# Later low parts, summed squares on TensorE, two scalings on ACT and pinned transposes in a two-layer trunk

## The chip, the cores and the metric

The kernel runs on one core of one Trainium2 chip. The metric is the device time of one execution in microseconds; of the kernel before, three runs were taken (2293.90, 2294.22 and 2296.38), and their median is 2294.22 us. A separate execution was profiled.

## The reference, cut to what matters

256 tokens of width 2048 go through two layers. Layer 0 mixes 8 heads of differential attention with 8 heads of a gated delta rule, layer 1 is a dilated attention with 16 heads; behind each stands an MLP of width 8192. All of it is float32.

```python
def l2_norm(x):                    # of q and k of the delta rule, per head of 128
    xf = x.astype(jnp.float32)
    return xf * lax.rsqrt(jnp.sum(xf * xf, axis=-1, keepdims=True) + NORM_EPS)

def squared_relu_mlp(h, w1, w2):
    return jnp.square(jax.nn.relu(h @ w1)) @ w2

for l in range(DEPTH):
    i = l // 2
    if l % 2 == 0:
        x = x + diff_delta_mixer(rms_norm(x, ab_norm[i]), l, ...)
    else:
        x = x + dilated_mixer(rms_norm(x, c_norm[i]), ...)
    x = x + squared_relu_mlp(rms_norm(x, mlp_norm[l]), mlp_w1[l], mlp_w2[l])
```

In the mixer of layer 0, `bq` and `bk` are normed by `l2_norm` before the delta rule, and the output of the attention is normed per head (`rms_norm(oa, a_sub_norm)`).

## The kernel before, in words

**The dense products.** `dense` (L191) computes one block of up to 512 output columns for both halves of the tokens (h = 0, 1; 128 tokens each) over 16 chunks of 128 input channels (8, 10 or 6 chunks in the output projections). Activations and weights are split into a high part, rounded to the format fp32r, and a low part, the rest; a product is high by high, high by low and low by high. So each chunk has six instructions on TensorE: for each h, L210 (`sh` by `wh`), L211 (`sh` by `wl`, the weights' low part) and L212 (`sl` by `wh`), all added up in one bank of PSUM per h. ACT makes `wh` by a copy (L204), DVE then makes `wl` by a subtraction (L107 through `tt`). With `unit=2`, in the MLPs, one cast and one subtraction serve two chunks; with `unit=1`, everywhere else, each chunk has its own. Six buffers of `wh` and `wl` exist at `unit=1`, three double ones at `unit=2`. Weights come by DMA on SP's queue, two chunks at a time (`wload`).

**The streams.** Everything that is not a dense product is written as generators in three streams ("g" for the delta rule, "s" for the rest, "o" for the outputs). After every chunk (or every second one), `drip` runs one step of one of them, g and s in turn, "o" after each fourth. `flush` runs the steps without dense products between them.

**The order on the engines.** A planner takes the instructions in program order as their priority (casts and subtractions of weights are moved forward by AHEAD = 60), estimates when operands and buffers are ready, and fixes the order of each engine's queue from that. An instruction on TensorE can so be placed before products that come earlier in the program, where the planner expects those to wait. `tc.issue_after(ins)` forbids that: each instruction written in its block, on the engine of `ins`, is placed behind `ins`. `behind` (L400) wraps each step of a generator so, behind the dense product written last (`last_mm`). Before the change it stands inside the first mixer and is used for the first transposes of x alone.

**The delta rule.** `gdn` (L617) runs four times (s = 0 to 3), each for two heads in two halves of the tokens, which makes four tiles of 128 x 128. It reads `qk`, with channels in the partitions. It transposes the four tiles of k and the four of q into two banks of PSUM (L631, recorded under L235); ACT squares each tile with a sum along the row (L634, recorded under L125) and copies k to `kh` (L636); DVE makes the reciprocal root (`rsqrt`), scales the four tiles of `kh` (L641, recorded under L117), and the decay matrix `dd` follows. Three yields later `kh` is transposed again (`kt`, L658).

**The attention's output.** `diff_out` (L838) norms a block of four tiles: squares and sums on ACT, `rsqrt` and four scalings on DVE (L842, under L117), then transposes (`out_T`).

**The transitions.** `next_norm` (L295) makes the sums of squares and the transposed, split blocks of x for the next stage, one call for each quarter n of the width. For n = 3 three yields lie between the sums and the transposes, so that they are written among the chunks of the next stage's first dense block. Three such transitions exist: into the first MLP (`xb`), into the mixer of layer 1 (`xc`) and into the second MLP (`xd`). At each, the pool with the weights' casts changes, and the first cast of the new stage waits for the last dense product of the old one.

Of the kernel before, what the change touches and what calls it, by code (L numbers as in the profile page):

```python
# [11 lines left out]
F32 = mybir.dt.float32  # L12
# [3 lines left out]
ALU = mybir.AluOpType  # L16
# [3 lines left out]
P = 128  # L20
# [67 lines left out]
def trunk(  # L88
# [32 lines left out]
    def act(o, a, f, scale=1.0, bias=0.0, accum=None):  # L121
        if accum is None:
            S.activation(out=o, in_=a, func=f, scale=scale, bias=bias)  # L123
        else:
            S.activation(out=o, in_=a, func=f, scale=scale, bias=bias, accum_out=accum)  # L125
# [4 lines left out]
    def ps_t(name):  # L130
        return pst.tile([P, 512], F32, tag="t", name=name)
# [4 lines left out]
    def quads(t, n=4):  # L136
        return t.rearrange("p (c d) -> p c d", c=n)
# [53 lines left out]
    def dense(wsrc, stat, kcs, nm, pre=(), every=1, unit=1):  # L191

        n = sum(s.shape[1] for s in wsrc)
        ps = [psd.tile([P, 512], F32, tag="d", name=f"{nm}p{h}") for h in range(NH)]
        first, last = kcs[0], kcs[-1]
        for j, kc in enumerate(kcs):
            if j % 2 == 0:
                raw = pre[j // 2] if j // 2 < len(pre) else wload(wsrc, kc, nm)
            if j % unit == 0:
                w = raw[:, j % 2:j % 2 + unit, :n]  # L200
                whs = wq[0].tile([P, unit, 512], F32R, tag="wh", name=f"{nm}h{kc}", bufs=6 // unit)[:, :, :n]
                wls = wq[0].tile([P, unit, 512], F32R, tag="wl", name=f"{nm}l{kc}", bufs=6 // unit)[:, :, :n]
                with tc.high_priority(offset=AHEAD):
                    cast[0] = S.copy(whs, w)  # L204
                    tt(wls, w, whs.bitcast(F32), ALU.subtract)
            wh, wl = whs[:, j % unit], wls[:, j % unit]
            for h in range(NH):
                sh, sl = stat(kc, h)
                o = ps[h][:, :n]
                E.matmul(o, lhsT=sh, rhs=wh, start=kc == first, stop=False)  # L210
                E.matmul(o, lhsT=sh, rhs=wl, start=False, stop=False)  # L211
                last_mm[0] = E.matmul(o, lhsT=sl, rhs=wh, start=False, stop=kc == last)  # L212
            if j % every == 0:
                drip()
        return ps
# [18 lines left out]
    def transpose(o, i, k=P):  # L234
        E.transpose(o, i, ident[:k, :k])  # L235
# [51 lines left out]
    def turn_quadrant(src, dst, i):  # L287
# [3 lines left out]
        for j in range(4):  # L291
            dv = dst[32 * j:32 * j + 32].rearrange("p c (h t) -> p h c t", h=NH)
            V.transpose(out=dv[:, :, :, q], in_=sv[:, :, :, j, :])  # L293

    def next_norm(n, norm, nm, dst, pool=None):  # L295

        stats_block(xs[n], n, nm + "s")
        if n == 3:
            for _ in range(3):
                yield  # L300
        yield from xt_block(xs[n], n, norm, nm, dst, pool if n < 3 else None)
        if n == 3:
            stats_end(nm + "e")
            yield
# [73 lines left out]
    with ExitStack() as mix:  # L378
# [16 lines left out]
        def xt_blocks():  # L395
            for n in range(4):
                for _ in xt_block(xq[n], n, 0, f"xa{n}", xb):
                    yield

        def behind(gen):  # L400

            while True:
                with tc.issue_after(last_mm[0].ins):
                    if next(gen, gen) is gen:
                        return
                yield

        blocks = xt_blocks()
        next(blocks)
# [207 lines left out]
        def gdn(qks, s, vb, nm):  # L617

            def mt(tag, n=4, share=None):
                return mp.tile([P, n, P], F32, tag="g_" + (share or tag), name=nm + tag)  # L620
# [2 lines left out]
                yield  # L623
            qk = qks[s]
            tiles = [(h, e) for h in range(NH) for e in range(2)]
            ssq = mp.tile([P, 8], F32, tag="g_ss", name=nm + "ss")
            kh = mt("kh")
            for w, o, c in (("k", 0, 2), ("q", 4, 0)):
                pt = ps_t(nm + w + "p")
                for i, (h, e) in enumerate(tiles):  # L630
                    transpose(pt[:, i * P:(i + 1) * P], qk[:, c + e, h * P:(h + 1) * P])  # L631
                j = sp.tile([P, 512], F32, tag="junk", name=f"{nm}j{o}")
                for i in range(4):
                    act(j[:, i * P:(i + 1) * P], pt[:, i * P:(i + 1) * P], AF.Square, accum=ssq[:, o + i:o + i + 1])  # L634
                if w == "k":
                    S.copy(kh, quads(pt))  # L636
            yield
            rs = mp.tile([P, 8], F32, tag="g_rs", name=nm + "rs")
            rsqrt(rs, ssq, 8, 1.0, nm)
            for i in range(4):  # L640
                ts(kh[:, i, :], kh[:, i, :], rs[:, i:i + 1], None, ALU.mult)  # L641
            sq = mp.tile([P, 4], F32, tag="g_sq", name=nm + "sq")
            ts(sq, rs[:, 4:8], 128.0 ** -0.5, None, ALU.mult)

# [5 lines left out]
                hd = 2 * s + e  # L650
                stt(dd[:, i, :], dd[:, i, :], gc[:, h, hd:hd + 1], cst("causal"), ALU.add, ALU.min)
            act(dd, dd, AF.Exp)
            for _ in range(3):
                yield
            khT, kd, kbg = mt("khT"), mt("kd", n=2), mt("kbg", n=2)
            t = ps_t(nm + "kt")
# [181 lines left out]
        def diff_out(o, s, nm):  # L838
            rs = mp.tile([P, 4], F32, tag="o_rs", name=nm + "ors")
            rsqrt(rs, out_ss(o, nm), 4, 1.0 / 128.0, nm + "o")  # L840
            for i in range(4):
                ts(o[:, i, :], o[:, i, :], rs[:, i:i + 1], None, ALU.mult)  # L842
            yield
            yield
            out_T(o, nm, oa, s, gsub)
            yield
# [355 lines left out]
```

## Time and profile before

| | before |
|---|---|
| median of three runs | 2294.22 us |
| the profiled execution's own time | 2293.58 us |
| its span, first to last instruction | 2291.8 us |
| TensorE (PE) busy, instructions | 2279.2 us, 10536 |
| weight loads (PEld) busy | 1887.6 us |
| VectorE (DVE) busy | 1670.6 us, 3027 |
| ScalarE (ACT) busy | 1195.0 us, 1865 |
| DMA, mean | 186 GB/s |

"Busy" is the share of the span in which an engine had an instruction in work. TensorE's instructions are pipelined: the record of a dense product is 0.39 us long, and the next one starts before it ends. What a product takes from the time is so read from the distance of two starts, in the timeline. A transpose is one record on TensorE; a product of float32 operands that are not rounded to fp32r is two records, each with a weight load of its own.

### The profile page before, as it was taken

The numbers are of one execution on the slowest core, as the hardware profiler recorded it, in microseconds if no ns is written. First come the engines' busy times: TensorE is split into PE (matmuls) and PEld (weight loads), VectorE is DVE, ScalarE is ACT, GpSimd is POOL, SyncE is SP. The second block draws the span as 40 slices with busy tenths as digits, with TensorE's granted clock in tenths as the row PEclk, the third lists the DMA queues.
The fourth block names the chain that finished last, engine by engine and source line by source line (L and its number), as shares of the span: only waits on it lengthen the run. The fifth ranks groups of instructions, "written<-read, shape, count | busy, mean of one in ns | idle before, by whom it ended". The sixth has DMA issues, their size and how long they took to land.

```text
span 2291.8 us, 29876 instructions
## 1 busy us (share of the span) xinstructions
PE 2279.2 (99%) x10536; PEld 1887.6 (82%) x10536; DVE 1670.6 (73%) x3027; ACT 1195.0 (52%) x1865; POOL 5.6 (0%) x15
## 2 busy tenths in 40 slices
PE   9999999999999999999999999999999999999999
PEld 8887888788888888888888888888888888888887
DVE  6868797867757746846888888986775775775774
ACT  6557666655534534534545565555543543543553
POOL 0000000000000000000000000000000000000000
PEclk9999999999999999999999999999999999999999
DMA  8655564456666666666656555555666666666665
GB/s 259 192 172 159 143 182 134 141 177 199 200 194 186 200 194 189 197 195 190 194 192 193 183 176 176 174 184 168 194 194 194 194 194 194 191 195 194 188 208 165
DMA packets 271546, 426.54 MB, mean 186 GB/s; under 512 B 22386, under 2 KB 102436, under 8 KB 271396
## 3 DMA queue, kind: packets, MB, share of 16 engines
q1 hardware_dynamic: 271220, 424.57, 61.3%
q8 instruction: 82, 1.34, 0.3%
q14 instruction: 68, 0.56, 0.1%
q10 hardware_dynamic: 176, 0.07, 0.0%
HBM read 420.11 MB, written 4.46 MB: 185 GB/s over the span
## 4 chain that ended last, share of the span: by engine, by line
PE 94%; DVE 3%; DMA 1%; ACT 1%; issue 1%; SPq 0%; ACTq 0%
PE m_0p L211 3%; PE n_2p L211 3%; PE n_1p L212 3%; PE n_0p L212 3%; PE m_3p L212 3%; PE m_3p L210 3%; PE m_2p L212 3%; PE m_2p L210 3%; PE m_1p L212 3%; PE m_1p L210 3%; PE n_0p L210 3%; PE n_1p L211 3%; PE n_2p L212 3%; PE m_0p L212 3%; PE n_2p L210 3%; PE n_1p L210 3%
## 5 line engine op out<-in xcount | busy, mean ns | idle before, releaser
L107 DVE TENSOR_TENSOR n_3l<-n_3r,n_3h 128x1024 fp32r<-128x1024 f32 x64 | 78.4, 1224 | 76.8 <-ACT n_3h L204 76.7
L107 DVE TENSOR_TENSOR n_2l<-n_2r,n_2h 128x1024 fp32r<-128x1024 f32 x64 | 78.4, 1224 | 76.8 <-ACT n_2h L204 76.7
L107 DVE TENSOR_TENSOR m_0l<-m_0r,m_0h 128x1024 fp32r<-128x1024 f32 x64 | 78.1, 1225 | 73.4 <-ACT m_0h L204 73.0
L107 DVE TENSOR_TENSOR n_1l<-n_1r,n_1h 128x1024 fp32r<-128x1024 f32 x64 | 78.4, 1224 | 67.7 <-ACT n_1h L204 66.9
L204 ACT CAST n_2h<-n_2r 128x1024 fp32r<-128x1024 f32 x64 | 67.5, 1054 | 100.2 <-PE n_2p L212 59.9
L204 ACT CAST n_3h<-n_3r 128x1024 fp32r<-128x1024 f32 x64 | 67.5, 1054 | 100.2 <-PE n_3p L212 59.9
L204 ACT CAST m_0h<-m_0r 128x1024 fp32r<-128x1024 f32 x64 | 67.1, 1054 | 97.2 <-PE m_0p L212 59.9
L204 ACT CAST n_1h<-n_1r 128x1024 fp32r<-128x1024 f32 x64 | 67.5, 1054 | 92.8 <-PE n_1p L212 59.9
L107 DVE TENSOR_TENSOR m_1l<-m_1r,m_1h 128x1024 fp32r<-128x1024 f32 x64 | 78.4, 1225 | 36.9 <-ACT m_1h L204 35.9
L204 ACT CAST m_1h<-m_1r 128x1024 fp32r<-128x1024 f32 x64 | 67.5, 1054 | 66.6 <-PE m_1p L212 38.3
L204 ACT CAST m_3h<-m_3r 128x1024 fp32r<-128x1024 f32 x64 | 67.5, 1054 | 57.3 <-PE m_3p L212 39.9
L204 ACT CAST n_0h<-n_0r 128x1024 fp32r<-128x1024 f32 x64 | 67.5, 1054 | 57.3 <-PE n_0p L212 39.9
L204 ACT CAST m_2h<-m_2r 128x1024 fp32r<-128x1024 f32 x64 | 67.5, 1054 | 57.3 <-PE m_2p L212 39.9
L107 DVE TENSOR_TENSOR n_0l<-n_0r,n_0h 128x1024 fp32r<-128x1024 f32 x64 | 78.4, 1225 | 25.8 <-ACT n_0h L204 24.0
L107 DVE TENSOR_TENSOR m_3l<-m_3r,m_3h 128x1024 fp32r<-128x1024 f32 x64 | 78.4, 1225 | 25.7 <-ACT m_3h L204 23.9
L107 DVE TENSOR_TENSOR m_2l<-m_2r,m_2h 128x1024 fp32r<-128x1024 f32 x64 | 78.4, 1225 | 25.7 <-ACT m_2h L204 23.7
L293 DVE STREAM_TRANSPOSE m_0hT<-m_0r 32x256 f32<-32x256 f32 x128 | 55.8, 436 | 5.8 <-ACT m_0r L123 3.7
L293 DVE STREAM_TRANSPOSE m_1hT<-m_1r 32x256 f32<-32x256 f32 x128 | 55.8, 436 | 5.7 <-ACT m_1r L123 3.6
L293 DVE STREAM_TRANSPOSE m_2hT<-m_2r 32x256 f32<-32x256 f32 x128 | 55.8, 436 | 5.7 <-ACT m_2r L123 3.6
L293 DVE STREAM_TRANSPOSE m_3hT<-m_3r 32x256 f32<-32x256 f32 x128 | 55.8, 436 | 5.7 <-ACT m_3r L123 3.6
L210 PE MATMUL n_0p<-n_0h,m_0hh 128*128 128x512 f32 x64 | 24.9, 389 | 0.0
L211 PE MATMUL n_0p<-n_0l,m_0hh 128*128 128x512 f32 x64 | 24.9, 389 | 0.0
(2553 smaller groups left out, 7388.3 us busy)
## 6 DMA issues: line engine op xcount, KB each, us to landing
m_0r<-in_mlp_w_dram SPq DMA_DIRECT2D x64, 512.0 KB, 4.2
m_1r<-in_mlp_w_dram SPq DMA_DIRECT2D x64, 512.0 KB, 3.8
m_2r<-in_mlp_w_dram SPq DMA_DIRECT2D x64, 512.0 KB, 4.2
m_3r<-in_mlp_w_dram SPq DMA_DIRECT2D x64, 512.0 KB, 3.8
n_0r<-in_mlp_w_dram SPq DMA_DIRECT2D x64, 512.0 KB, 4.2
n_1r<-in_mlp_w_dram SPq DMA_DIRECT2D x64, 512.0 KB, 4.2
n_2r<-in_mlp_w_dram SPq DMA_DIRECT2D x64, 512.0 KB, 4.3
n_3r<-in_mlp_w_dram SPq DMA_DIRECT2D x64, 512.0 KB, 4.3
```

The source lines that it names most:

```text
L107: V.tensor_tensor(out=o, in0=a, in1=b, op=op)
L204: cast[0] = S.copy(whs, w)
L210: E.matmul(o, lhsT=sh, rhs=wh, start=kc == first, stop=False)
L211: E.matmul(o, lhsT=sh, rhs=wl, start=False, stop=False)
L212: last_mm[0] = E.matmul(o, lhsT=sl, rhs=wh, start=False, stop=kc == last)
L293: V.transpose(out=dv[:, :, :, q], in_=sv[:, :, :, j, :])
```

## The change

Four things are changed. In `dense`, L211 leaves its place: for each chunk, both halves' L210 and L212 come first, and the products with `wl` follow; at `unit=1` they follow one chunk later (the last two chunks' at the end), at `unit=2` in the same chunk. In `gdn`, the squares of q and k are made by one ACT instruction over the untransposed `qk`, and eight products with a column of ones sum them; q is transposed no more, k is transposed two steps later, and ACT scales it on its way out of PSUM. In `diff_out`, the four scalings go from DVE to ACT. `behind` moves to the outer function, and for n = 3 `next_norm` has one yield in place of three and runs the steps of the transposes behind the dense product written last.

```diff
         ps = [psd.tile([P, 512], F32, tag="d", name=f"{nm}p{h}") for h in range(NH)]
-        first, last = kcs[0], kcs[-1]
+        first, last, lows = kcs[0], kcs[-1], deque()
...
                 E.matmul(o, lhsT=sh, rhs=wh, start=kc == first, stop=False)
-                E.matmul(o, lhsT=sh, rhs=wl, start=False, stop=False)
-                last_mm[0] = E.matmul(o, lhsT=sl, rhs=wh, start=False, stop=kc == last)
+                last_mm[0] = E.matmul(o, lhsT=sl, rhs=wh, start=False, stop=False)
+
+            lows.append((kc, wl))
+            while len(lows) > (unit == 1 and kc != last):
+                kl, wl = lows.popleft()
+                for h in range(NH):
+                    last_mm[0] = E.matmul(ps[h][:, :n], lhsT=stat(kl, h)[0], rhs=wl, start=False, stop=kl == last)
...
+    def behind(gen):
+
+        while True:
+            with tc.issue_after(last_mm[0].ins):
+                if next(gen, gen) is gen:
+                    return
+            yield
+
     def next_norm(n, norm, nm, dst, pool=None):
 
         stats_block(xs[n], n, nm + "s")
         if n == 3:
-            for _ in range(3):
-                yield
-        yield from xt_block(xs[n], n, norm, nm, dst, pool if n < 3 else None)
+            yield
+            yield from behind(xt_block(xs[n], n, norm, nm, dst))
+        else:
+            yield from xt_block(xs[n], n, norm, nm, dst, pool)
...
-            ssq = mp.tile([P, 8], F32, tag="g_ss", name=nm + "ss")
-            kh = mt("kh")
-            for w, o, c in (("k", 0, 2), ("q", 4, 0)):
-                pt = ps_t(nm + w + "p")
+
+            q2 = mp.tile([P, 4, T], F32, tag="xy", name=nm + "q2")
+            act(q2, qk, AF.Square)
+            yield
+            ssq = ps_m(nm + "ss")
+            for o, c in ((0, 2), (4, 0)):
                 for i, (h, e) in enumerate(tiles):
-                    transpose(pt[:, i * P:(i + 1) * P], qk[:, c + e, h * P:(h + 1) * P])
-                j = sp.tile([P, 512], F32, tag="junk", name=f"{nm}j{o}")
-                for i in range(4):
-                    act(j[:, i * P:(i + 1) * P], pt[:, i * P:(i + 1) * P], AF.Square, accum=ssq[:, o + i:o + i + 1])
-                if w == "k":
-                    S.copy(kh, quads(pt))
-            yield
+                    E.matmul(ssq[:, o + i:o + i + 1], lhsT=q2[:, c + e, h * P:(h + 1) * P], rhs=cst("ones")[:, :1],
+                             start=True, stop=True)
             rs = mp.tile([P, 8], F32, tag="g_rs", name=nm + "rs")
-            rsqrt(rs, ssq, 8, 1.0, nm)
-            for i in range(4):
-                ts(kh[:, i, :], kh[:, i, :], rs[:, i:i + 1], None, ALU.mult)
+            rsqrt(rs, ssq[:, :8], 8, 1.0, nm)
...
             act(dd, dd, AF.Exp)
-            for _ in range(3):
+            yield
+            kh = mt("kh")
+            pt = ps_t(nm + "kp")
+            for i, (h, e) in enumerate(tiles):
+                transpose(pt[:, i * P:(i + 1) * P], qk[:, 2 + e, h * P:(h + 1) * P])
+            for i in range(4):
+                act(kh[:, i, :], pt[:, i * P:(i + 1) * P], AF.Identity, scale=rs[:, i:i + 1])
+            for _ in range(2):
                 yield
...
             rsqrt(rs, out_ss(o, nm), 4, 1.0 / 128.0, nm + "o")
             for i in range(4):
-                ts(o[:, i, :], o[:, i, :], rs[:, i:i + 1], None, ALU.mult)
+                act(o[:, i, :], o[:, i, :], AF.Identity, scale=rs[:, i:i + 1])
```

## Rows read from the trace of the kernel before

**Rows 1.** The table of windows: for each stretch of the span its length, then busy time and instructions of PE, PEld, DVE, ACT and POOL, the granted TensorE clock, the DMA share and GB/s. The stretches are the mixer of layer 0, the first MLP and the mixer of layer 1.

```profile
7.20:510.70 503.50, 499.08 (x2611) 413.40 (x2611) 388.61 (x1063) 320.28 (x764) 4.37 (x9) 1.00 0.59 174
510.70:1209.30 698.60, 698.06 (x3081) 577.51 (x3080) 489.60 (x637) 332.70 (x352) 0.00 (x0) 1.00 0.64 193
1209.30:1589.30 380.00, 379.73 (x1745) 315.59 (x1744) 325.43 (x749) 214.26 (x416) 0.00 (x0) 1.00 0.58 179
```

**Rows 2.** The waits of PE over the whole span: who waited for whom, us in total, times, longest. Five of the twelve lines.

```profile
PE b0p L210 <- ACT xa0h L123: 1.6, 1, 1.6
...
PE d1t L235 <- DVE d1qk L107: 1.2, 1, 1.2
PE d2ot L235 <- DVE d2o L117: 1.1, 1, 1.1
...
PE g1kt L235 <- DVE g1kh L117: 0.5, 1, 0.5
PE m_0p L211 <- DVE m_0l L107: 0.4, 2, 0.2
```

**Rows 3.** The timeline of the last microseconds: start, length, engine, line, operation, tiles, shapes, count, and in brackets the idle time before and what ended it. The second MLP's last dense products, the addition to x and the output.

```profile
2287.00 0.39 PE L212 MATMUL n_3p<-n_3h,m_3hl 128*128 128x512 f32 x1
...
2287.42 1.37 DVE L107 TENSOR_TENSOR xs<-n_3p,xs 128x512 f32<-128x512 f32 x2 [5.17 <-PE n_3p L212]
2287.45 0.39 PE L211 MATMUL n_3p<-n_3l,m_3hh 128*128 128x512 f32 x1
2287.68 0.39 PE L212 MATMUL n_3p<-n_3h,m_3hl 128*128 128x512 f32 x1
2288.14 1.03 SPq L1173 DMA_DIRECT2D out_dram<-xs  x2
```

**Rows 4.** PE's timeline around the transposes of k and q in the fourth delta rule.

```profile
376.27 0.60 PE L235 MATMUL g3kp<-ca,qk 128*128 128x128 f32 x4
376.70 0.60 PE L235 MATMUL g3qp<-ca,qk 128*128 128x128 f32 x4
377.06 0.48 PE L210 MATMUL a3p<-a3h,xa1h 128*128 128x512 f32 x1
377.37 0.40 PE L211 MATMUL a3p<-a3l,xa1h 128*128 128x512 f32 x1
```

**Rows 5.** PE's timeline around two float32 products of 128 x 128 stationary elements with 16 moving columns (the sums of the gates; two records each), and around eight records with 64 x 64 stationary elements and 64 columns.

```profile
77.25 0.29 PE L538 MATMUL pgc<-gg,ca 128*128 128x16 f32 x2
77.39 0.37 PE L539 MATMUL pgc<-gg,ca 128*128 128x16 f32 x2
77.61 0.47 PE L210 MATMUL b1p<-b1h,xa1h 128*128 128x512 f32 x1
77.93 0.39 PE L211 MATMUL b1p<-b1l,xa1h 128*128 128x512 f32 x1
...
160.15 0.68 PE L761 MATMUL g0lyz<-g0xy,g0Pz 64*64 64x64 f32 x8
160.76 0.50 PE L210 MATMUL a0p<-a0h,xa2h 128*128 128x512 f32 x1
```

**Rows 6.** The timeline of the transition into the first MLP (weight loads left out).

```profile
510.51 0.39 PE L212 MATMUL wo13p<-wo13h,d3ol 128*128 128x512 f32 x1
510.98 2.95 ACT L204 CAST m_0h<-m_0r 128x1024 fp32r<-128x1024 f32 x3 [4.04 <-PE wo13p L212]
511.01 0.44 PE L235 MATMUL xb3t<-ca,xs 128*128 128x128 f32 x2
511.69 0.55 PE L235 MATMUL xb3t<-ca,xs 128*128 128x128 f32 x3 [0.24 <-DVE xs L107]
...
512.08 0.74 PE L210 MATMUL m_0p<-m_0h,xb0h 128*128 128x512 f32 x2
512.66 0.49 PE L235 MATMUL xb3t<-ca,xs 128*128 128x128 f32 x3
...
513.34 0.50 PE L211 MATMUL m_0p<-m_0l,xb0h 128*128 128x512 f32 x1 [0.19 <-DVE m_0l L107]
513.67 0.39 PE L212 MATMUL m_0p<-m_0h,xb0l 128*128 128x512 f32 x1
...
514.37 0.40 PE L210 MATMUL m_0p<-m_0h,xb0h 128*128 128x512 f32 x1
```

**Rows 7.** The timeline of the transition into the mixer of layer 1.

```profile
1209.11 0.39 PE L212 MATMUL n_3p<-n_3h,m_3hl 128*128 128x512 f32 x1
...
1210.21 0.73 PE L210 MATMUL c0p<-c0h,xc0h 128*128 128x512 f32 x2 [0.17 <-ACT c0h L204]
...
1212.04 0.40 PE L210 MATMUL c0p<-c0h,xc0h 128*128 128x512 f32 x1
```

**Rows 8.** Groups of ACT and DVE by line (line, engine, operation, tiles, shapes, count, busy us, mean ns of one, idle before): a square with its sum and the reading of the sum, the copy of k, a function over 128 x 1024 elements, and a scaling out of PSUM on ACT.

```profile
L125 ACT ACTIVATE g3j<-g3kp 128x128 f32<-128x128 f32 x4 | 1.0, 274 | 0.0
L636 ACT COPY g3kh<-g3kp 128x512 f32<-128x512 f32 x1 | 0.6, 602 | 0.0
L123 ACT ACTIVATE c3x<-qk 128x1024 f32<-128x1024 f32 x1 | 1.1, 1062 | 0.0
L123 ACT ACTIVATE g3o<-g3po,g3sq 128x128 f32<-128x128 f32 x2 | 0.7, 364 | 0.1
```

More of the change, by code (lines that the diff above doesn't have):

```diff
@@ L398, in xt_blocks @@
                     yield
[L400 to L405, printed above, removed]
-                yield
         blocks = xt_blocks()
@@ L625, in gdn @@
             tiles = [(h, e) for h in range(NH) for e in range(2)]
-            ssq = mp.tile([P, 8], F32, tag="g_ss", name=nm + "ss")
-            kh = mt("kh")
-            for w, o, c in (("k", 0, 2), ("q", 4, 0)):
-                pt = ps_t(nm + w + "p")
-                for i, (h, e) in enumerate(tiles):
-                    transpose(pt[:, i * P:(i + 1) * P], qk[:, c + e, h * P:(h + 1) * P])
-                j = sp.tile([P, 512], F32, tag="junk", name=f"{nm}j{o}")
-                for i in range(4):
-                    act(j[:, i * P:(i + 1) * P], pt[:, i * P:(i + 1) * P], AF.Square, accum=ssq[:, o + i:o + i + 1])
-                if w == "k":
-                    S.copy(kh, quads(pt))
-            yield
+            q2 = mp.tile([P, 4, T], F32, tag="xy", name=nm + "q2")
[3 more added lines that the diff above has]
+            for o, c in ((0, 2), (4, 0)):
+                for i, (h, e) in enumerate(tiles):
+                    E.matmul(ssq[:, o + i:o + i + 1], lhsT=q2[:, c + e, h * P:(h + 1) * P], rhs=cst("ones")[:, :1],
+                             start=True, stop=True)
             rs = mp.tile([P, 8], F32, tag="g_rs", name=nm + "rs")
-            rsqrt(rs, ssq, 8, 1.0, nm)
-            for i in range(4):
-                ts(kh[:, i, :], kh[:, i, :], rs[:, i:i + 1], None, ALU.mult)
+            rsqrt(rs, ssq[:, :8], 8, 1.0, nm)
             sq = mp.tile([P, 4], F32, tag="g_sq", name=nm + "sq")
```

## The prediction

> **What bounds the kernel now.** I read the table of windows first. The reader is to see how little of TensorE's time is open: in the mixer of layer 0 PE is busy 499.08 of 503.50 us, in the first MLP 698.06 of 698.60, in the mixer of layer 1 379.73 of 380.00, all at the full granted clock of 2.4 GHz, while DVE and ACT have time to spare in each [rows 1]. So the end is set by the number of instructions on PE and by what each takes, and the open time is 4.4 us, 0.5 us and 0.3 us. Then the waits of PE: past the start, only single waits of 1.2 us and less are left, nearly all in the first mixer, and the wait for a low part of the weights, which the first edit is about, is listed with 0.4 us in all, at two transitions [rows 2]. Then the timeline, for the price of a record. The last products of the second MLP start 0.23 us apart (2287.45 to 2287.68, and 2287.00 to 2287.45 for two) [rows 3]. A group of small records inside a dense block is priced from its first start to the start of the dense product behind it, with what that product's own distance to the next has over 0.23.
>
> **Part 1, the low parts later.** The number of dense products stays. The waits that the new order can take away are those of L211 on DVE, 0.4 us at two transitions [rows 2], which part 4 counts. Whether a product's pace depends on its neighbours I read from the three kinds of succession there are: the same stationary block twice (L210 to L211), another low part (L211 to L212) and another bank of PSUM (L212 to L210 of the other half). They are all 0.22 to 0.23 us apart [rows 3, 6]; so the new succession is costed at nothing, between a loss and a gain of the same unknown size. One cost is sure: with the order of before, the first half's sum is ready three products before the second's, now one product before. At the very end of the kernel DVE adds both halves to x, 1.37 us together, from 2287.42, when the first half is ready [rows 3]. It will start two products later, so the end comes 2 x 0.23 = 0.45 us later. Elsewhere such an addition lies beside PE's next block.
>
> **Part 2, the squares of q and k.** Removed per delta rule: eight transposes, from 376.27 to 377.06, and the product behind them is 0.31 us from its successor, 0.08 over the usual: 0.87 us, 0.11 each [rows 4]. Added: four transposes of k in a group of their own, 0.44 us, and eight float32 products with one moving column. Such a product is two records: the two products of the gates' sums stand as four, each pair with 128 x 128 stationary elements and 16 moving columns [rows 5]. The four go from 77.25 to 77.61, and the product behind them is 0.09 over its usual distance: 0.45 us, 0.112 a record. Sixteen records make 1.80 us. One column in place of 16 can cost no more, so 0.112 is the upper bound; the lower one is nothing. Eight records with half as many stationary columns take 0.61 us, under 0.08 each [rows 5], so I think that the stationary block sets the price and take 0.112. Per delta rule that is 1.80 + 0.44 - 0.87 = 1.37 us, and four times 5.5 us, on the engine that sets the end. At the lower bound it is four times 0.44 - 0.87, which is -1.7 us.
>
> The Trainium skill, page "TensorE: Matmul & The Clock Gate", section "Part 1: The HAM clock gate", states that start to start never drops below about 25 ns however few columns a matmul has. By that floor alone the 64 records would take an estimated 1.6 us, and the part -0.1 us. The section "LDWEIGHTS (loading the stationary operand)" of that page has the load at P / 1.2, 107 ns for 128 columns; the trace's 0.112 us for 16 moving columns agrees with this one and not with the floor, since each record here brings its own load.
>
> On ACT, per delta rule, eight squares with their sums and the copy of k go; the squares follow each other every 0.25 us (1.0 us for four) and the copy takes 0.60, 2.6 us together. One square of 128 x 1024, 1.06 us, and four scalings out of PSUM, 0.36 us or less each, take their place, 2.5 us at most [rows 8]. ACT has 183 us open in this mixer [rows 1], so neither counts. The `q2` tile shares its buffer with `xy` of the delta rule before, which has ended by then, as the four run one after the other in one stream. The chain gets one more crossing between ACT and PE (square, sums, root, scaling), but the yields stay four; what may be late next is the second transposition of k, behind ACT's scalings and the casts queued there.
>
> **Part 3, two scalings on ACT.** The scalings of k and of the attention's output leave DVE. Two of PE's waits end on exactly these instructions (`d2ot` on L117, 1.1 us; `g1kt` on L117, 0.5 us) [rows 2]. Both could stay, since the root before them remains on DVE; at the other end all of the mixer's 4.4 us of open PE time could go [rows 1]. I take the two listed waits as gone, -1.6 us, and keep 0 and -4.4 as ends.
>
> **Part 4, the pinned transposes.** In the first MLP's transition, PE's last product of the mixer starts at 510.51, the cast of the new weights runs behind it, and the first new product starts at 512.08. The low part lets L211 start at 513.34. The eight transposes of `xb3` stand in these two holes [rows 6]: they cost nothing. By 514.37 the first chunk is done, 3.86 us after 510.51. Pinned, they come behind the products of chunks 3 and 5 and cost 8 x 0.11 = 0.87 us there. In the first hole nothing is left; in the second there are now four products with `wh` in place of two. So: 512.08, plus 0.33 for the first product behind a stop (513.34 to 513.67 [rows 6]) and three of 0.23, is 513.1; the low part is ready at 513.34; plus 0.33 and 0.23 is 513.90, plus the transposes 514.77. That is 0.40 us later than before. The transition into the second MLP has the same form; I take the same. In the one into the mixer of layer 1, the first product starts at 1210.21 and the first chunk is done at 1212.04 [rows 7]; with the low parts a chunk later no wait stays, so 1210.21 + 0.33 + 5 x 0.23 + 0.87 = 1212.55, 0.51 us later. Sum: +1.3 us; if the planner had other work for the holes, 0.
>
> **The sum.** +0.45 + 5.5 - 1.6 + 1.3 = +5.6 us. The profiled execution took 2293.58 us, 0.64 below the median of 2294.22; the changed kernel's profiled execution would take 2299.2, its median 2299.8 us. What a measurement of this kernel can tell from no change is 0.2%, 4.6 us: 2289.6 to 2298.8.
>
> **The rivals.**
> 1. *Not slower, since one column costs next to nothing.* The mechanism is the load of the squares' block, hidden behind the record before. For it: the loads of the dense products are hidden so, as 0.23 us is about 512 columns' own time at 2.4 GHz (0.213). Against it: 16 columns cost 0.112 us [rows 5]. At nothing per record the sum is 5.6 - 7.2 = -1.6 us, 2292.6 us; at 0.03 it is 2294.5. It decides below 0.096 us a record, where the sum falls under 4.6. The floor that the Trainium skill's page states would put it here.
> 2. *The waits of the first mixer go altogether.* For it: DVE and ACT have less to do in the chain. Against it: the roots and most of the other waits are not touched. -4.4 in place of -1.6: 2297.0 us.
> 3. *New waits.* The planner lays out the first mixer anew, and the extra crossing of ACT and PE puts the second transposition of k, or what hangs on it, in front of ready products. For it: waits of 0.5 to 1.2 us stand there now, from estimates that were not met [rows 2]. Four more of 1.2 us: 2304.6 us.
> 4. *The change does not do what it says to the pace.* If the new succession of products shifts their distance by one nanosecond, some 9500 products make 9.5 us, either way: 2290 or 2309. The equal distances [rows 3] speak against it.
>
> **How the numbers follow.** My forecast has 0.50 with its own range of 2297 to 2303; rival 1 has 0.16, rival 2 0.17, rival 3 0.12, rival 4 0.05. Slower by over 0.2%: 0.40 of the forecast's 0.50, rival 3, half of rival 4, 0.54. Faster by over 0.2%: it needs more than 10 us against part 2, while the first mixer has 4.4 us open; 0.02 each from rival 1 and rival 4 and 0.01 from rival 2, 0.05. Within: 0.41. The range reaches from 2293.5 (rival 1 with a small price) to 2305.5 (rival 3).
>
> **What would show it.** Part 2: the eight products stand as 16 records about 0.11 us apart in the timeline, in each of four groups; closer than 0.096, and rival 1 holds. The mixer's window grows by about 4 us, the MLPs' by less than 1 each with their products still 0.23 apart; another distance is rival 4. Part 3: no wait of `d2ot` or `g1kt`. Part 4: PE stands still from 510.7 to the first new product, and the transposes of `xb3` lie between chunks 3 and 6. The end: 0.45 us more between the last product and the last instruction. I am wrong if the mixer's window does not grow, or if its idle time grows by more than 2 us.

## The result and the profile after

The changed kernel takes 2303.11 us (median of seven executions, 2300.44 to 2305.10). The kernel before, run beside it, takes 2294.12 us (seven, 2293.70 to 2296.38). The ratio is 1.0038, with an interval of 1.0028 to 1.0048: the change makes the kernel slower by 0.4%, more than the 0.2% that can be told from nothing. The prediction said slower, 2299.8 us: the range of 2293.5 to 2305.5 holds the time, the forecast's own range of 2297 to 2303 just misses it. The profiled execution took 2300.48 us, where the prediction had 2299.2.

The first table to read is that of the windows: the mixer of layer 0, the first MLP and the mixer of layer 1 of the changed kernel, cut at the first product of the one and the first of the next.

```profile
7.15:514.52 507.37, 501.44 (x2659) 417.94 (x2659) 382.89 (x1030) 324.24 (x732) 4.38 (x9) 1.00 0.58 172
514.52:1214.30 699.78, 698.53 (x3082) 577.19 (x3080) 488.12 (x636) 329.55 (x352) 0.00 (x0) 1.00 0.63 193
1214.30:1594.90 380.60, 379.84 (x1746) 315.71 (x1744) 326.04 (x749) 213.98 (x416) 0.00 (x0) 1.00 0.57 179
```

Beside [rows 1], PE has 2.4 us more work and 1.5 us more open time in the first mixer, and each other stretch has grown by 0.6 to 1.2 us. The waits of PE, four of the ten lines, name the new open time.

```profile
PE m_0p L210 <- ACT m_0h L204: 2.4, 2, 1.2
PE c2t L240 <- ACT g1aT L741: 1.8, 1, 1.8
...
PE d2ot L240 <- ACT d2o L123: 1.3, 1, 1.3
...
PE c0p L210 <- ACT c0h L204: 0.7, 1, 0.7
```

`g1kt` of [rows 2] is gone, `d2ot` has stayed with ACT in DVE's place, and `c2t`, `m_0p` (L210) and `c0p` have come or grown.

Finer cuts, made at the starts of single products (the first of the mixer, the last of `wo13p`, the first of the second MLP block `m_1p`, the last of `n_3p`, and so on), put the difference of the two profiled executions in its places:

| stage | before | after | change | predicted |
|---|---|---|---|---|
| start to first product | 7.21 | 7.15 | -0.06 | 0 |
| first mixer | 503.31 | 507.34 | +4.03 | +3.9 |
| into the first MLP | 24.27 | 24.83 | +0.56 | +0.40 |
| first MLP | 674.33 | 674.92 | +0.59 | 0 |
| into the mixer of layer 1 | 23.75 | 23.98 | +0.23 | +0.51 |
| mixer of layer 1 | 356.21 | 356.23 | +0.02 | 0 |
| into the second MLP | 24.27 | 24.79 | +0.52 | +0.40 |
| second MLP | 674.33 | 674.93 | +0.60 | 0 |
| last product to the end | 4.10 | 4.51 | +0.41 | +0.45 |
| span | 2291.78 | 2298.70 | +6.92 | +5.6 |

**The squares** stand as forecast. PE's timeline in the first delta rule:

```profile
89.17 0.62 PE L217 MATMUL b1p<-b1l,xa3h 128*128 128x512 f32 x2
89.64 1.84 PE L639 MATMUL g0ss<-ca,g0q 128*128 128x1 f32 x16
91.34 0.48 PE L210 MATMUL b1p<-b1h,xa3h 128*128 128x512 f32 x1
91.65 0.40 PE L211 MATMUL b1p<-b1h,xa3l 128*128 128x512 f32 x1
```

Sixteen records of one moving column take 1.70 us to the product behind them, whose own distance to its successor is 0.08 over the usual 0.23: 1.78 us, 0.111 a record. The moving side is a single column, and the price is that of 16 columns [rows 5].

**The new wait.** The timeline around `c2t`, all engines:

```profile
225.77 0.60 PE L240 MATMUL c2t<-ca,b2raw 128*128 128x128 f32 x4
225.89 0.35 DVE L113 SCALAR_TENSOR_TENSOR g2dd<-g2dd,gc,ca 128x128 f32<-128x128 f32 x1 [1.35 <-DMA g2dd<-scg]
226.16 0.15 DVE L113 SCALAR_TENSOR_TENSOR d0ors<-d0oq,d0ors 128x4 f32<-128x4 f32 x1
...
226.41 1.28 ACT L123 ACTIVATE d0o<-d0o,d0ors 128x128 f32<-128x128 f32 x4 [2.12 <-DVE d0ors L113]
...
227.59 0.56 ACT L741 COPY g1aT<-g1tt 128x512 f32<-128x512 f32 x1
...
228.21 0.66 PE L240 MATMUL c2t<-ca,b2raw 128*128 128x128 f32 x4 [1.84 <-ACT g1aT L741]
```

It is read backwards. PE at 228.21 waits for the copy `g1aT`, which empties the bank of PSUM that the transposes need. The copy's source, the four transposes `g1tt`, was begun at 223.93 and took 0.60 us, but on ACT it stands behind the four scalings of `d0o`, and these wait 2.12 us for the last step of the root `d0ors`. That step of 0.15 us stands on DVE behind `g2dd`, which waits for a DMA. Three queues in order hand one late transfer on to PE.

**The transition into the first MLP**, PE's timeline:

```profile
513.82 1.07 PE L217 MATMUL wo13p<-wo13l,d3oh 128*128 128x512 f32 x4
516.06 0.50 PE L210 MATMUL m_0p<-m_0h,xb0h 128*128 128x512 f32 x1 [1.18 <-ACT m_0h L204]
516.40 0.39 PE L211 MATMUL m_0p<-m_0h,xb0l 128*128 128x512 f32 x1
516.63 0.40 PE L210 MATMUL m_0p<-m_0h,xb0h 128*128 128x512 f32 x1
516.87 0.39 PE L211 MATMUL m_0p<-m_0h,xb0l 128*128 128x512 f32 x1
517.32 0.73 PE L217 MATMUL m_0p<-m_0l,xb0h 128*128 128x512 f32 x2
```

The hole is as long as before, the transposes have left it [rows 6], and four products stand ahead of the low part, as forecast.

**The MLPs**, which were costed at nothing, lose here, four times in each:

```profile
619.86 1.22 DVE L107 TENSOR_TENSOR m_3hl<-m_3hT,m_3hh 128x1024 fp32r<-128x1024 f32 x1
...
620.92 0.39 PE L210 MATMUL n_0p<-n_0h,m_3hh 128*128 128x512 f32 x1
...
621.13 0.19 PEld L211 LDWEIGHTS n_0p<-n_0h,m_3hl 128*128 128x128 f32 x1 [0.25 <-DVE m_3hl L107]
621.15 0.49 PE L211 MATMUL n_0p<-n_0h,m_3hl 128*128 128x512 f32 x1
621.48 0.40 PE L210 MATMUL n_0p<-n_0h,m_3hh 128*128 128x512 f32 x1
```

The product with the low part of the last hidden block is now the second of its chunk, not the third, and so needs that low part 0.23 us sooner. From 621.15 to 621.48 are 0.33 us in place of 0.23. Elsewhere two products are 0.23 us apart, as before.

### The profile page after: what moved, and what is told of

Read it like the earlier page. It is cut to its first block, busy times and chain, and to the rows that moved or that the text cites. A ratio compares the mean times of both kernels' runs of the same rounds, so it can differ in the third digit from the quotient of the medians.

```text
span 2298.7 us, 30262 instructions
## 1 busy us (share of the span) xinstructions
PE 2282.8 (99%) x10584; PEld 1892.2 (82%) x10584; DVE 1662.8 (72%) x2995; ACT 1191.8 (52%) x1833; POOL 5.6 (0%) x15
## 4 chain that ended last, share of the span: by engine, by line
PE 97%; DVE 1%; DMA 1%; ACT 1%; issue 0%; SPq 0%; DVEq 0%; ACTq 0%
PE n_0p L211 3%; PE m_0p L217 3%; PE n_0p L217 3%; PE n_2p L211 3%; PE n_3p L211 3%; PE n_1p L211 3%; PE m_2p L211 3%; PE m_3p L211 3%; PE m_1p L211 3%; PE n_0p L210 3%; PE m_2p L217 3%; PE n_1p L217 3%; PE m_3p L217 3%; PE m_1p L217 3%; PE n_2p L217 3%; PE m_1p L210 3%
## 5 line engine op out<-in xcount | busy, mean ns | idle before, releaser
L211 PE MATMUL n_0p<-n_0h,m_3hl 128*128 128x512 f32 x64 | 25.8, 404 | 0.0
L210 PE MATMUL n_0p<-n_0h,m_3hh 128*128 128x512 f32 x64 | 25.0, 391 | 0.0
```

## The experiments

Twelve kernels were run. All changes of time are against the kernel before, run on the same chip beside them.

**1. Parts alone, and the change without one.** The first kernel has the whole change with the old transitions:

```diff
         if n == 3:
-            yield
-            yield from behind(xt_block(xs[n], n, norm, nm, dst))
-        else:
-            yield from xt_block(xs[n], n, norm, nm, dst, pool)
+            for _ in range(3):
+                yield
+        yield from xt_block(xs[n], n, norm, nm, dst, pool if n < 3 else None)
```

> The changed kernel with its transitions as before (transposes not pinned). Theory A, that pinning leaves TensorE standing at the three transitions, which costs 1.3 us in every execution and in many of them lowers the granted clock for a stretch after: the time falls to about 2299, all executions within some 2 us. Theory B, that the scatter of the changed kernel (2300.4 to 2305.1) comes from the first mixer's new order and its 1.8 us wait: the time falls by 1.3 us alone, to about 2302, and the scatter of 4 to 5 us stays.

Measured: 2302.09 us, +9.1 (ratio 1.0044, 1.0030 to 1.0058). That is no less than the changed kernel's +9.0, and the five executions lie 2.8 us apart, between what the two theories said. In the profiled execution the transitions do come back (24.21, 23.88 and 24.17 us, 1.3 us less in sum than in the changed kernel's), but the first mixer takes 508.57 us, 1.2 us more. Two lines of PE's waits:

```profile
PE c2t L240 <- ACT g1aT L740: 2.8, 1, 2.8
...
PE xb3t L240 <- DVE xs L107: 0.6, 1, 0.6
```

`c2t` waits a microsecond longer than in the changed kernel, which is most of what the mixer lost. The wait of `xb3t`, which `xc3t` and `xd3t` have too, lies inside the transitions and is the first edit's, as the run with the low parts alone, below, has the same three: the first half's sum is ready two products later, the addition to `xs` follows it, and here a transpose waits for that. Pinned, the transposes no longer wait for `xs`, and yet by these two traces the transitions are 1.3 us longer with the pins. That the pins gain anything together with the late low parts is not shown.

The second has the pins alone, put into the kernel before, with `behind` moved to the outer function:

```diff
-            for _ in range(3):
-                yield
-        yield from xt_block(xs[n], n, norm, nm, dst, pool if n < 3 else None)
+            yield
+            yield from behind(xt_block(xs[n], n, norm, nm, dst))
+        else:
+            yield from xt_block(xs[n], n, norm, nm, dst, pool)
```

> The kernel before with the pinned transposes alone. Theory A: the lowest times at about 2295.5 (1.3 to 1.8 us more, as the low parts still stand between the others here), but a scatter of 3 to 5 us above that and a median near 2298. Theory B: 2295.5 to 2296 with no more scatter than the kernel before.

Measured: 2296.68 us, +3.7 (1.0019, 1.0010 to 1.0028); the eleven executions reach from 2294.79 to 2301.46 us, and the profiled one, 2299.47, is the second longest. In it the transitions into the MLPs grew from 24.27 to 26.83 and 26.87 us, 2.56 and 2.60. The windows around the first of them show why it is more than the 0.87 us of eight transposes (granted clock third from the end):

```profile
513.00:515.00 2.00, 1.47 (x5) 1.16 (x5) 2.00 (x3) 2.00 (x5) 0.00 (x0) 0.63 0.25 32
515.00:517.00 2.00, 2.00 (x6) 1.61 (x5) 1.79 (x8) 0.37 (x2) 0.00 (x0) 0.52 0.92 296
517.00:519.00 2.00, 2.00 (x10) 1.62 (x10) 0.40 (x3) 1.05 (x1) 0.00 (x0) 1.00 0.97 342
```

And PE's timeline there:

```profile
512.29 0.73 PE L210 MATMUL m_0p<-m_0h,xb0h 128*128 128x512 f32 x2 [1.18 <-ACT m_0h L204]
513.55 0.79 PE L211 MATMUL m_0p<-m_0l,xb0h 128*128 128x512 f32 x1 [0.53 <-DVE m_0l L107]
514.14 0.63 PE L212 MATMUL m_0p<-m_0h,xb0l 128*128 128x512 f32 x1
514.57 0.63 PE L211 MATMUL m_0p<-m_0l,xb0h 128*128 128x512 f32 x1
```

PE stands 1.18 us and then 0.53 us without the transposes that filled these two holes, and the granted clock falls to half, 1.2 GHz: the products are 0.43 us apart. The stretch lasts 3.4 us and costs half of that, 1.7 us. What is left, 0.86 and 0.9 us, is the eight transposes. With 0.51 us in the transition into the mixer of layer 1 that makes 2.3 us at full clock, and the two half-clock stretches add 3.4; the median of +3.7 lies between. With the new order of products the second hole is shorter, and in the changed kernel's trace the clock stays full there.

The third has the squares of q and k alone, the whole hunk of `gdn`; its core:

```diff
-                    transpose(pt[:, i * P:(i + 1) * P], qk[:, c + e, h * P:(h + 1) * P])
...
+            act(q2, qk, AF.Square)
...
+                    E.matmul(ssq[:, o + i:o + i + 1], lhsT=q2[:, c + e, h * P:(h + 1) * P], rhs=cst("ones")[:, :1],
+                             start=True, stop=True)
```

> The kernel before with the summed squares and the scaling of k on ACT alone. By the sum, 64 records of 0.112 us less 16 transposes of 0.109 us: 5.5 us more, 2299.6, if no wait comes or goes, and 2298 to 2301 with the waits. Theory A: scatter as before (under 3 us). Theory B: scatter of 4 to 5 us, if the delta rule's order is its source.

Measured: 2297.79 us, +4.8 (1.0025, 1.0015 to 1.0036), against a term of +5.5. Priced by its records, the part costs four times 1.78 + 0.44 - 0.87, 5.4 us. The wait of `g1kt`, 0.5 us, is gone with this edit, so it belongs here, while `g3ot` waits 1.9 us in its place. In all, the open time of the first mixer is 1.7 us longer than in the trace of before (6.1 against 4.4). So 4.8 is not the price of the records alone: they and the new waits make 7.1, and the mixer's other work on PE must have taken some 2 us less. Where, no run takes apart.

The fourth has the low parts alone, the whole hunk of `dense`; its core:

```diff
-                E.matmul(o, lhsT=sh, rhs=wl, start=False, stop=False)
...
+            lows.append((kc, wl))
+            while len(lows) > (unit == 1 and kc != last):
+                kl, wl = lows.popleft()
+                for h in range(NH):
+                    last_mm[0] = E.matmul(ps[h][:, :n], lhsT=stat(kl, h)[0], rhs=wl, start=False, stop=kl == last)
```

> The kernel before with the low parts' products later alone, transposes not pinned. By the sum: 0.45 us more at the end, 0.8 us more for eight products of n_0p that now wait 0.1 us for the low part of the hidden block, 0.3 to 0.9 us less at the two transitions into the MLPs, and the waits of the first mixer laid out anew: 2293 to 2296, scatter as before under theory A.

Measured: 2295.00 us, +2.0 (1.0007, 0.9999 to 1.0016, so nothing at all is just not excluded). In its trace the MLPs grew by 0.56 and 0.55 us, the end by 0.43, the transitions by between -0.08 and +0.12: alone, this edit gains next to nothing in any of these stages.

The fifth has the attention's scalings alone.

```diff
             for i in range(4):
-                ts(o[:, i, :], o[:, i, :], rs[:, i:i + 1], None, ALU.mult)
+                act(o[:, i, :], o[:, i, :], AF.Identity, scale=rs[:, i:i + 1])
```

> The kernel before with the attention's scaling on ACT alone. My prediction took about 1.1 us less for it (the wait of d2ot). Theory C: ACT waits for DVE's roots in front of other work, 0 to 3 us more than before. Theory D: within 1 us of before.

Measured: 2293.71 us, +0.2 (1.0000, 0.9991 to 1.0009): nothing, and `c2t` is not among its waits. Alone, the four parts make 3.7 + 4.8 + 2.0 + 0.2 = 10.7 us, where the change as a whole makes 9.0. The intervals of the single parts are some 2 us wide to each side, so the difference of 1.7 is not clear of noise. One place where the parts do not add up is seen in the traces: together with the new order the pins cost the transitions 1.3 us, and the half clock of the run with the pins alone is not there.

**2. The changed kernel again, and without the scalings on ACT.** The first is the changed kernel as it is.

> The changed kernel again, beside its variants on the same chip: 7 to 9 us over the kernel before, executions spread over 4 to 5 us.

Measured: 2302.28 us (2300.78 to 2305.99), +8.8 (1.0044, 1.0030 to 1.0058). The second has the lines of the last diff the other way round.

> The changed kernel with the attention's scaling back on DVE. Theory C, that the scaling on ACT makes ACT's queue wait for DVE's root (2.1 us idle before the first d0o scaling), with the copy of g1aT behind it, and PE behind that (c2t, 1.8 us): the wait of c2t is gone and the time falls by 1.5 to 3 us against the changed kernel. Theory D, that the wait comes from the new layout of the first mixer as a whole: another wait of the same size, the time within 1 us.

Measured: 2300.49 us, +7.0 (1.0031, 1.0019 to 1.0044), 1.8 less than the changed kernel beside it; the lowest executions differ by 1.1 (2299.69 and 2300.78). With five executions of each the two intervals overlap, so the time alone does not decide; the list of waits does. `c2t` is no longer among the waits, while `d2ot` is:

```profile
PE d2ot L240 <- DVE d2o L117: 1.3, 1, 1.3
```

So the new wait needs the scalings on ACT, though not them alone, since the run with nothing but the scalings moved has no `c2t`; and the old wait was never theirs. Why `d2ot` stays is seen on DVE, in the timeline of the changed kernel:

```profile
418.72 0.14 DVE L107 TENSOR_TENSOR d2oq<-d2ors 128x4 f32<-128x4 f32 x1
...
418.88 0.67 DVE L107 TENSOR_TENSOR wo01l<-wo01r,wo01h 128x512 fp32r<-128x512 f32 x1
419.48 0.14 DVE L113 SCALAR_TENSOR_TENSOR d2oq<-d2oq,d2oz 128x4 f32<-128x4 f32 x1
...
419.64 0.67 DVE L107 TENSOR_TENSOR wo01l<-wo01r,wo01h 128x512 fp32r<-128x512 f32 x1
420.24 0.14 DVE L113 SCALAR_TENSOR_TENSOR d2ors<-d2oq,d2ors 128x4 f32<-128x4 f32 x1
```

In the last six of its eleven steps the root, 0.14 us a step, has a subtraction of weights of 0.67 us behind each, so it goes on once in 0.76 us. Moving the scalings leaves that as it is. And what is saved is small. The groups of the scalings' tile, before and after (duration min/median/max in ns, first and last start), first the kernel before:

```profile
L117 DVE TENSOR_SCALAR d2o<-d2o,d2ors x4: 268/270/271, 417.3 to 417.9; 128x128 f32<-128x128 f32 x4
```

Then the changed kernel:

```profile
L123 ACT ACTIVATE d2o<-d2o,d2ors x4: 386/386/402, 420.4 to 421.3; 128x128 f32<-128x128 f32 x4
```

On ACT the four take 0.9 us from first to last start, on DVE 0.6.

**3. Fillers in the transitions.** The executions of the changed kernel lie 5 us apart, and the mean granted clock goes along with the time: of the twelve in both sets, the six above 2302.5 us have 0.998 or 0.999, and the six below have 1.0. This run puts useless transposes into the holes of the three transitions.

```diff
+    def fill(n, nm):
+        t = ps_m(nm)
+        with tc.issue_after(last_mm[0].ins):
+            for _ in range(n):
+                transpose(t[:, :P], ident)
...
+        fill(10, f"fl{layer}")
         for g in range(4):
...
+        fill(6, "flc")
         for s in range(8):
```

> The changed kernel with useless transposes of the identity in the holes of the three transitions (ten, six and ten of 0.109 us). Theory A, that standing still there lowers the granted clock for a stretch in many executions: the lowest time stays within 0.5 us of the changed kernel's, the median falls by 1 to 2.5 us, and the profile shows no stretch at half the clock at 514 or 1595 us. Theory B, that the scatter has another source: median and scatter as in the changed kernel.

Measured: 2305.32 us (2299.78 to 2305.78), +11.8 (1.0047, 1.0035 to 1.0060, which overlaps with that of the changed kernel beside it). The holes are filled and their waits gone, and yet four of the five executions have a mean clock of 0.998 or 0.999 and lie above 2304 us. So filling these holes does not take the spread away, and standing still there is not what it needs.

**4. The first cast in halves.** The kernel before, with one edit: at the first dense block of each MLP the cast and the subtraction for the first two chunks are made chunk by chunk.

```diff
-                    cast[0] = S.copy(whs, w)
-                    tt(wls, w, whs.bitcast(F32), ALU.subtract)
+                    for u in [slice(i, i + 1) for i in range(unit)] if cut and j == 0 else [slice(0, unit)]:
+                        cast[0] = S.copy(whs[:, u], w[:, u])
+                        tt(wls[:, u], w[:, u], whs[:, u].bitcast(F32), ALU.subtract)
```

> The kernel before, with one edit: in the first dense block of each MLP the first cast and the first subtraction, which serve two chunks of weights (128 x 1024), are cut into two of one chunk each (128 x 512). Theory: what is open at the transition into an MLP is the time until the first high part and then until the first low part, and it goes with the size of these two instructions, not with the place of the transposes. The first product then starts about 0.5 us after the last product of the mixer plus one cast of half the size, near 0.6 us earlier than before, and the first low part is ready about 0.6 us after it in place of 1.26. The two transitions lose about 0.7 us each, 22.9 to 23.7 us in place of 24.27 from the last product of the mixer to the second block, the rest of the kernel is unchanged, and the time falls by 1.4 us, within what the measurement can tell from nothing. Rival: the eight transposes that stand in the holes now move behind products, so the transitions stay within 0.2 us of before.

Measured: 2292.93 us, -1.0 (0.9996, 0.9987 to 1.0005). The two transitions took 23.77 and 23.81 us, 0.50 and 0.46 less than before, just short of the expected range, which began at 0.57 less. PE's timeline shows both holes short and the transposes still in them:

```profile
510.02 0.44 PE L236 MATMUL xb3t<-ca,xs 128*128 128x128 f32 x2
510.67 0.73 PE L211 MATMUL m_0p<-m_0h,xb0h 128*128 128x512 f32 x2 [0.21 <-ACT m_0h L205]
511.24 0.49 PE L236 MATMUL xb3t<-ca,xs 128*128 128x128 f32 x3
511.49 0.47 PE L212 MATMUL m_0p<-m_0l,xb0h 128*128 128x512 f32 x1
```

Of all the kernels run it alone has a median under that of the kernel before, but the interval does not exclude that nothing changed.

**5. The start.** In the trace of the kernel before, PE waits 1.6 us ahead of the first product [rows 2], and behind it the clock is at half, as the window there shows:

```profile
7.70:11.10 3.40, 3.40 (x12) 2.72 (x11) 2.06 (x4) 1.96 (x4) 0.00 (x0) 0.50 1.05 377
```

The next run puts fourteen useless transposes into that wait.

```diff
         next(blocks)
+        for _ in range(14):
+            transpose(pw[:, :P], ident)
```

> The kernel before, with one edit: fourteen useless transposes of the identity stand on PE between the first four transposes of x and the first dense product, where PE waits 1.6 us in the trace of before. Theory: the scatter of the executions (2291 to 2296 us for the kernel before) comes from the first microseconds, where the granted clock falls to half behind this wait (7.7 to 11.1 us in the trace of before) in some executions; without the wait no half clock follows, the start takes 0 to 0.3 us longer and the mixer of layer 0 1.7 us less than in that trace, and the executions lie within 2 us of the lowest. Rival: the clock falls for another reason or elsewhere; then the executions scatter over 4 us as before, and the median stays within 0.5 us.

The window behind the first product of this run:

```profile
8.10:11.20 3.10, 3.10 (x15) 2.40 (x16) 2.54 (x6) 1.93 (x4) 0.00 (x0) 1.00 1.07 396
```

Measured: 2294.27 us, +0.4 (1.0004, 0.9995 to 1.0012). The eleven executions lie within 2.0 us (2293.59 to 2295.63), those of the kernel before beside it within 4.3 (21, 2291.86 to 2296.20). That speaks for the start as a good part of the scatter of the kernel before. It is no proof: the eleven executions of the run with the scalings alone, without this filling, lie within 2.6 us. The start can differ in two ways: in the eleven traces without fillers there the first product comes between 7.07 and 8.25 us, and four of the eleven have half pace behind it. With them it comes between 7.82 and 8.10. The median did not fall: in this trace the first product comes at 8.10, and new waits of the mixer (`g1ly` 1.1 us, a second of `d1t`) stand against the gain.

The same filling in the changed kernel:

> The changed kernel with fourteen useless transposes between the first four transposes of x and the first dense product, as in the run with the kernel before and this filling, where the executions came to lie within 2.0 us of each other. The changed kernel's own executions lie 5 us apart. Theory: of these 5 us the start makes 2 to 3, as in the kernel before, and the rest follows on the long wait of the second half of the first mixer (c2t, 1.8 us, behind ACT's scalings of the attention's output), which this kernel still has: the lowest execution is 1 to 2 us higher than the changed kernel's, 2301.5 to 2302.5, and the highest is still 4 us or more above the lowest. Rival: the start alone makes the scatter; then the executions lie within 2 us of each other, at 2301 to 2304.

Measured: 2299.51 us (eight, 2298.36 to 2302.08), +6.9 (1.0030, 1.0019 to 1.0040). And with the scalings back on DVE besides:

> The same kernel, with the scalings of the attention's output back on DVE, so that the wait of c2t is gone. Theory: without this wait and with the start filled, the executions lie within 2 us of each other, at 2300.5 to 2302.5, with the median 1 to 2 us under that of the run beside it. Rival: if the transitions with their pinned transposes, 1.2 us without work on PE each, are what lets the clock fall in some executions, the scatter is 4 us here too.

Measured: 2298.04 us (ten, 2297.71 to 2300.61), +5.4 (1.0025, 1.0015 to 1.0034). The levels of both were missed: the lowest execution of the first was expected above that of the changed kernel and came 2 us below it. The step from the first to the second, 1.5 us, is as expected, though the intervals overlap. With the start filled the mixer is laid out otherwise: `c2t` waits 0.6 us in the first of the two, where 1.8 was counted on. So the pair does not tell the wait's part in the scatter from the start's. Beside their counterparts without the filling, the spreads go from 5.2 us (the changed kernel's repetition, five executions) to 3.7, but from 1.3 us (the run with the scalings back on DVE, five) to 2.9: that the filling narrows the changed kernel's spread is not shown. The loss against the kernel before goes from 8.8 us to 6.9, and from 7.0 to 5.4, again with intervals that overlap.

## Why the prediction was right, and where it was not

**Part 1, the low parts.** The pace is unchanged, so rival 4 falls, and the end came 0.41 us later where 0.45 was worked out. What failed is that no cost beside the end was looked for ("One cost is sure"). "Elsewhere such an addition lies beside PE's next block" holds in the changed kernel, but in the run with the low parts alone the transposes at the transitions wait 0.6 us for that addition. The new order also asks for the activations' low part one product sooner, and there DVE was just in time: 0.1 us, four times in each MLP, 0.4 of the 0.6 us that each lost; the rest was not traced. Alone, the edit measured +2.0 us, with an interval that begins just under nothing, and 0.45 had been counted.

**Part 2, the squares.** The price is right, in mechanism and size: 0.111 us a record where 0.112 was taken, and 1.78 us per delta rule where 1.80 was. That the part alone measured +4.8 us where 5.5 was worked out is less of a hit than it looks: 1.7 us more open time and some 2 us less of other work stand in it, neither of them in the working. Rival 1, which had one column cost next to nothing, falls. The Trainium skill (page "TensorE: Matmul & The Clock Gate", section "LDWEIGHTS (loading the stationary operand)") prices the load of 128 stationary columns at 107 ns; the 0.111 us here agrees with it, and the floor of about 25 ns in the page's section on the clock gate is not what a record with a load of its own costs.

**Part 3, the scalings.** This step failed: "I take the two listed waits as gone, -1.6 us". Only `g1kt` went, 0.5 us, and that with part 2. `d2ot` waits 1.3 us where it waited 1.1, since the root ahead of the scalings, not the scalings, is late. With 1.5 us more open time in the mixer, the part lies outside both ends that were kept, 0 and -4.4, and rival 2 falls. And ACT, with its 183 us open, was taken to cost nothing. It has time, but keeps its order: a scaling that waits for DVE holds up the copy behind it, and so PE for 1.8 us. This is rival 3 in kind, with one wait in place of four, and behind another instruction than the second transposition of k. The measured median of 2303.1 us lies nearer to that rival's 2304.6 than to the forecast's 2299.8.

**Part 4, the pinned transposes.** The three transitions lost 0.56, 0.23 and 0.52 us, 1.31 in sum, and 1.3 had been worked out. The mechanism is as in the working: into the first MLP, the first chunk is done 3.39 us after the mixer's last product, as worked out, and the eight transposes stand behind the chunks foreseen. The sum is luck in part: the two MLPs' transitions lost 0.16 and 0.12 us more than the 0.40, the other 0.28 less than its 0.51. Alone, with the old order, the pins cost 3.7 us: half clock behind the empty holes had not been thought of.

**The sum.** The first mixer's +4.03 looks like the predicted +3.9, but by accident. In the trace of before, 1.6 us of this stage were lost to the half clock behind the start (the first product to the first transpose of `xa1`: 6.29 us, against 4.72 in the run with the scalings alone, which has the same order there and a full clock). Without them the mixer grew by 5.6 us: 4.1 of work and 1.5 of open time, where 5.5 and -1.6 had been worked out. As the records of part 2 make 5.4, the mixer's other work must have shrunk by 1.3 us; no run shows where. Of the 6.92 us of span, then, 5.6 are the mixer, less 1.6 for the clock, 1.3 the transitions, 1.2 the MLPs and 0.4 the end. The median's difference is 2.1 us larger than that of the spans, as the changed kernel's profiled execution is one of its lowest. So the median's +9.0, against +5.6 forecast, holds 2.1 us that no trace places. Where the clock fell in the longer executions no trace shows, as every profiled execution of the changed kernel had a mean clock of 1.0: that stays open.

"I am wrong if the mixer's window does not grow, or if its idle time grows by more than 2 us": it grew, and the idle time by 1.5.

## What to carry to other kernels

A float32 product of one column costs TensorE as much as a transpose of a full block, so, where TensorE sets the end, sums over partitions by products with ones pay only if they replace at least as many records. Ahead of moving work from the engine that a wait names, read what that engine was waiting for itself: here it was a root in eleven small steps, the last six each with a long subtraction behind it. Idle time of an engine says little about what can be put on it; an instruction that waits there holds up everything behind it.

## What the hardware showed

- **The granted clock fell to 1.2 GHz behind short open stretches, and not in each execution.** With the pins alone 1.2 us and 0.5 us of open time were followed by 3.4 us at half, in the changed kernel's trace 1.2 us and 0.2 us by none. Behind the start, four of the eleven traces without fillers there show half pace, none of the three with them. In these four PE had stood still for 1.6 to 2.2 us ahead of the first product, in the other seven for 0.6 to 1.8: the length alone does not tell.
- **The column of the clock can miss it.** In the trace of the low parts alone the products of the first microseconds are 0.43 us apart, as in the half-clock stretch of the run with the pins alone, and the column says 1.00. The windows:

```profile
11.00:12.00 1.00, 1.00 (x4) 0.81 (x4) 0.65 (x2) 0.47 (x1) 0.00 (x0) 1.00 1.07 414
12.00:13.00 1.00, 1.00 (x4) 0.81 (x3) 0.46 (x2) 0.76 (x2) 0.00 (x0) 1.00 1.04 389
```

And PE's timeline in them:

```profile
11.83 0.63 PE L210 MATMUL b0p<-b0h,xa0h 128*128 128x512 f32 x1
12.26 0.63 PE L211 MATMUL b0p<-b0h,xa0l 128*128 128x512 f32 x1
```

The distance of two products is the surer reading of the pace.
